# Parameters loaded as rows and turned by VectorE, and phases of three loads and three stores, in a batch normalisation that streams 1 GB

## The chip, the cores and the metric

The kernel runs on one core of one Trainium2 chip. SyncE, ScalarE, VectorE and GpSimd are engines of the core that run its program; the profile calls them SP, ACT, DVE and POOL. The data are moved by sixteen DMA engines, which work off what SyncE, ScalarE and GpSimd put on their queues. The metric is the device time of an execution in microseconds (us), lower is better. The span that the profile gives is about 2 us shorter than the measured time of the same execution.

## The reference

```python
# x: 32 x 256 x 128 x 128 float32; gamma, beta, running_mean, running_var: 256 float32
return gamma * (x - mean) / np.sqrt(var + eps) + beta      # parameters broadcast over the channel axis
```

With scale = gamma / sqrt(var + eps) and shift = beta - mean * scale it is one multiply and one add for each element. 537 MB are read and 537 MB written.

## The kernel before

A tile is 128 channels by 16384 elements, 8.39 MB, 64 KB in each partition. There are 64 tiles and three buffers. All big loads and stores are issued from SyncE's queue in the order of the program. A load waits until the store out of its buffer has landed, and a store waits for VectorE.

```python
for i in range(NBUF):            # NBUF = 3
    issue_load(i)                # nc.sync.dma_start(out=t, in_=xr[i])

def load_param(ap_1d):           # four of these, on GpSimd's queue
    t = params.tile([P, NCB], mybir.dt.float32, tag=ap_1d.tensor.name)
    nc.gpsimd.dma_start(out=t, in_=ap_1d.rearrange("(j p) -> p j", p=P))
    return t
# ... sqrt on ScalarE, reciprocal, two multiplies and a subtract on VectorE: scale_t, shift_t ...

# compute(i): nc.vector.tensor_scalar in place, t = t * scale_t + shift_t
K = NBUF - 1                     # two
for b in range((NT + K - 1) // K):
    idxs = [i for i in range(K * b, K * b + K) if i < NT]
    for i in idxs:
        compute(i)
    for i in idxs:
        store(i)
    for i in idxs:
        issue_load(i + NBUF)
```

So the queue carries three loads and then, again and again, two stores and two loads.

Of the kernel before, what the change touches and what calls it, by code (L numbers as in the profile page):

```python
# [1 line left out]

# [4 lines left out]


SINGLE_QUEUE = True  # L10
NBUF = 3


@with_exitstack
def kernel(
    ctx: ExitStack,
    tc: tile.TileContext,
    x: bass.AP,
    gamma: bass.AP,
    beta: bass.AP,  # L20
    running_mean: bass.AP,
    running_var: bass.AP,
    out: bass.AP,
):
    nc = tc.nc
    eps = 1e-5

    N, C, H, W = x.shape
    P = nc.NUM_PARTITIONS
    assert C % P == 0  # L30
    NCB = C // P
    HW = H * W
    NT = N * NCB

    params = ctx.enter_context(tc.tile_pool(name="params", bufs=1))
    data = ctx.enter_context(tc.tile_pool(name="data", bufs=NBUF))

    xr = x.rearrange("n (cb p) h w -> (n cb) p (h w)", p=P)
    outr = out.rearrange("n (cb p) h w -> (n cb) p (h w)", p=P)

    tiles = {}
    loads = {}

    def issue_load(i):
        if i >= NT:
            return
        t = data.tile([P, HW], mybir.dt.float32, tag="t")
        loads[i] = nc.sync.dma_start(out=t[:], in_=xr[i])  # L48
        tiles[i] = t

    for i in range(NBUF):
        issue_load(i)

    def load_param(ap_1d):
        t = params.tile([P, NCB], mybir.dt.float32, tag=ap_1d.tensor.name)
        nc.gpsimd.dma_start(out=t, in_=ap_1d.rearrange("(j p) -> p j", p=P))  # L56
        return t

    var_t = load_param(running_var)
    gamma_t = load_param(gamma)  # L60
    beta_t = load_param(beta)
    mean_t = load_param(running_mean)

    eps_t = params.tile([P, 1], mybir.dt.float32, tag="eps")
    nc.vector.memset(eps_t, eps)  # L65

    scale_t = params.tile([P, NCB], mybir.dt.float32, tag="scale")
    shift_t = params.tile([P, NCB], mybir.dt.float32, tag="shift")
    tmp_t = params.tile([P, NCB], mybir.dt.float32, tag="tmp")

    nc.scalar.activation(  # L71
        out=tmp_t[:],
        in_=var_t[:],
        func=mybir.ActivationFunctionType.Sqrt,
        bias=eps_t[:],
        scale=1.0,
    )
    nc.vector.reciprocal(out=tmp_t[:], in_=tmp_t[:])  # L78
    nc.vector.tensor_mul(out=scale_t[:], in0=gamma_t[:], in1=tmp_t[:])  # L79
    nc.vector.tensor_mul(out=tmp_t[:], in0=mean_t[:], in1=scale_t[:])  # L80
    nc.vector.tensor_sub(out=shift_t[:], in0=beta_t[:], in1=tmp_t[:])  # L81

    def compute(i):
        t = tiles[i]
        cb = i % NCB
        nc.vector.tensor_scalar(  # L86
            out=t[:],
            in0=t[:],
            scalar1=scale_t[:, cb : cb + 1],
            scalar2=shift_t[:, cb : cb + 1],  # L90
            op0=mybir.AluOpType.mult,
            op1=mybir.AluOpType.add,
        )

    def store(i):
        t = tiles.pop(i)
        (nc.sync if SINGLE_QUEUE else nc.scalar).dma_start(out=outr[i], in_=t[:])  # L97

    K = NBUF - 1
    for b in range((NT + K - 1) // K):  # L100
        idxs = [i for i in range(K * b, K * b + K) if i < NT]
        for i in idxs:
            compute(i)
        for i in idxs:
            store(i)
        for i in idxs:
            issue_load(i + NBUF)


# [1 line left out]
_INS = ['x', 'gamma', 'beta', 'running_mean', 'running_var']  # L111
_OUTS = [((32, 256, 128, 128), 'float32')]


# [23 lines left out]
```

## Time and profile before

| what | value | where it is read |
|---|---|---|
| time, median of 3 runs | 2491.8 us | timed runs, 2489.71 to 2493.32 |
| span of the profiled execution | 2488.1 us | head of the page |
| data queue's share of 16 DMA engines | 99.8% | queue table |
| VectorE busy | 564.7 us, 23% | busy table |
| VectorE waiting for loads | 1867.9 us | groups by line |

The following lines are from the page of the kernel before. The first two give a DMA queue's packets, MB and share of 16 engines. The last is the group of the big VectorE operation: line, engine, operation, tiles, shapes and count; then busy us and mean ns; then idle us before it and what ended it.

```profile
q1 hardware_dynamic: 18432, 1073.75, 99.8%
q0 software_dynamic: 128, 0.00, 0.0%
...
L86 DVE TENSOR_SCALAR t<-t,scale_t,shift_t 128x16384 f32<-128x16384 f32 x64 | 564.0, 8812 | 1868.0 <-DMA t<-in_x_dram 1867.9
```

The reader should see that VectorE needs 8.8 us for each tile and waits more than three times as long as it works, while the data queue (q1) keeps all sixteen engines at work. Queue q0 carries the GpSimd parameter loads.

The start of the timeline of the kernel before; columns are start, length (us), engine, line, operation, and in brackets the idle time before it.

```profile
17.42 0.16 DVE L79 TENSOR_TENSOR scale_t<-t,tmp_t 128x2 f32<-128x2 f32 x1 [3.20 <-DMA t<-in_gamma_dram]
25.17 0.16 DVE L80 TENSOR_TENSOR tmp_t<-t,scale_t 128x2 f32<-128x2 f32 x1 [7.58 <-DMA t<-in_running_mean_dram]
...
25.56 8.81 DVE L86 TENSOR_SCALAR t<-t,scale_t,shift_t 128x16384 f32<-128x16384 f32 x1
34.40 19.06 SPq L97 DMA_DIRECT2D out_dram<-t  x2
44.28 8.81 DVE L86 TENSOR_SCALAR t<-t,scale_t,shift_t 128x16384 f32<-128x16384 f32 x1 [9.91 <-DMA t<-in_x_dram]
63.64 8.81 DVE L86 TENSOR_SCALAR t<-t,scale_t,shift_t 128x16384 f32<-128x16384 f32 x1 [10.55 <-DMA t<-in_x_dram]
```

The first big operation waits for the parameters until 25.56 us. But the store that it releases at 34.40 us stands in the queue behind loads 1 and 2, and load 2 ends at about 63.6 us. An earlier start would gain nothing. Loads 1 and 2 land 19.36 us apart.

The chain of waits of the kernel before, two pieces of it far apart (start, length, what):

```profile
82.93 38.59 DMA t<-in_x_dram
...
2409.84 38.69 DMA t<-in_x_dram
```

Between these are 30 cycles of two loads and two stores, (2409.84 - 82.93) / 30 = 77.56 us each.

### The profile page before, as it was taken

The page shows a single profiled execution, that of the slowest core. Times are in us where ns is not written, and L with a number is a line of the kernel's source. Part 1 is how long each engine was busy: PE and PEld are TensorE (multiplying, and loading weights), DVE is VectorE, ACT ScalarE, POOL GpSimd, SP SyncE. Part 2 cuts the span into 40 slices and gives each one's busy share as a digit, 9 for nine tenths or more (in the row PEclk, how much of TensorE's full clock was granted, in tenths as well). Part 3 has the DMA queues.
Part 4 walks back from the last instruction along what each step waited for, and adds up shares of the span by engine and source line. Part 5 has one row for each costly group of instructions (what it writes and reads, how often), then busy time and mean ns, then how long its engine had stood idle before and what let it go on. Part 6 is the DMA issues. An engine that isn't in the chain of part 4 may idle for free.

```text
span 2488.1 us, 378 instructions
## 1 busy us (share of the span) xinstructions
DVE 564.7 (23%) x69; ACT 1.6 (0%) x2; POOL 3.2 (0%) x8
## 2 busy tenths in 40 slices
DVE  2122211222112221122212222121221212212121
ACT  0000000000000000000000000000000000000000
POOL 0000000000000000000000000000000000000000
DMA  9999999999999999999999999999999999999998
GB/s 414 429 438 433 433 429 437 436 430 431 435 436 433 428 437 436 434 428 436 433 437 428 435 435 435 426 437 436 435 427 435 436 438 426 434 437 436 432 431 378
DMA packets 18562, 1073.77 MB, mean 432 GB/s; under 512 B 2176, under 2 KB 2176, under 8 KB 2176
## 3 DMA queue, kind: packets, MB, share of 16 engines
q1 hardware_dynamic: 18432, 1073.75, 99.8%
q0 software_dynamic: 128, 0.00, 0.0%
q14 instruction: 2, 0.02, 0.0%
HBM read 536.88 MB, written 536.87 MB: 432 GB/s over the span
## 4 chain that ended last, share of the span: by engine, by line
DMA 51%; another core or an unknown queue 36%; DVE 11%; SPq 0%; issue 0%; POOL 0%; DVEq 0%; POOLq 0%; PEldq 0%
DMA t<-in_x_dram 48%; DVE t L86 11%; DMA out_dram<-t 2%; DMA t<-in_running_mean_dram 1%; SPq L97 0%; POOL t L56 0%; DVEq L86 0%; POOLq L133 0%; SPq L48 0%; DVE shift_t L81 0%; DVE tmp_t L80 0%; DVEq L80 0%; PEldq L133 0%
## 5 line engine op out<-in xcount | busy, mean ns | idle before, releaser
L86 DVE TENSOR_SCALAR t<-t,scale_t,shift_t 128x16384 f32<-128x16384 f32 x64 | 564.0, 8812 | 1868.0 <-DMA t<-in_x_dram 1867.9
L78 DVE RECIPROCAL tmp_t<-tmp_t 128x2 f32<-128x2 f32 x1 | 0.2, 166 | 13.2 <-ACT tmp_t L71 13.2
L80 DVE TENSOR_TENSOR tmp_t<-t,scale_t 128x2 f32<-128x2 f32 x1 | 0.2, 160 | 7.6 <-DMA t<-in_running_mean_dram 7.6
L71 ACT ACT_TABLE_LOAD x1 | 1.3, 1283 | 12.4 <-DMA t<-in_running_var_dram 12.4
L79 DVE TENSOR_TENSOR scale_t<-t,tmp_t 128x2 f32<-128x2 f32 x1 | 0.2, 160 | 3.2 <-DMA t<-in_gamma_dram 3.2
L56 POOL DMA_DIRECT2D t<-in_running_var_dram x1 | 0.8, 839 | 0.8 <-PEq L133 0.8
L56 POOL DMA_DIRECT2D t<-in_gamma_dram x1 | 0.7, 722 | 0.0
L56 POOL DMA_DIRECT2D t<-in_beta_dram x1 | 0.7, 722 | 0.0
L56 POOL DMA_DIRECT2D t<-in_running_mean_dram x1 | 0.7, 722 | 0.0
L71 ACT ACTIVATE tmp_t<-t,eps_t 128x2 f32<-128x2 f32 x1 | 0.3, 295 | 0.0
L65 DVE MEMSET eps_t<- 128x1 f32 x1 | 0.1, 59 | 0.8 <-PEq L122 0.8
L81 DVE TENSOR_TENSOR shift_t<-t,tmp_t 128x2 f32<-128x2 f32 x1 | 0.2, 160 | 0.0
L122 POOL MEMSET const-bfloat16-1.0<- 128x1 bf16 x1 | 0.1, 96 | 0.0
L122 POOL MEMSET const-uint8-127<- 128x1 uint8 x1 | 0.1, 94 | 0.0
L122 POOL MEMSET const-float32-0.0<- 128x1 f32 x1 | 0.1, 93 | 0.2 <-issue 0.2
L122 POOL MEMSET const-float32-1.0<- 128x1 f32 x1 | 0.1, 93 | 0.0
## 6 DMA issues: line engine op xcount, KB each, us to landing
t<-in_x_dram SPq DMA_DIRECT2D x64, 38.6
out_dram<-t SPq DMA_DIRECT2D x64, 49.9
t<-in_running_var_dram POOLq DMA_DIRECT2D x1, 1.0 KB, 11.1
t<-in_gamma_dram POOLq DMA_DIRECT2D x1, 1.0 KB, 15.2
t<-in_beta_dram POOLq DMA_DIRECT2D x1, 1.0 KB, 19.5
t<-in_running_mean_dram POOLq DMA_DIRECT2D x1, 1.0 KB, 21.6
```

The source lines that it names most:

```text
L56: nc.gpsimd.dma_start(out=t, in_=ap_1d.rearrange("(j p) -> p j", p=P))
L65: nc.vector.memset(eps_t, eps)
L71: nc.scalar.activation(out=tmp_t[:], in_=var_t[:], func=mybir.ActivationFunctionType.Sqrt, bias=eps_t[:], scale=1.0,)
L78: nc.vector.reciprocal(out=tmp_t[:], in_=tmp_t[:])
L79: nc.vector.tensor_mul(out=scale_t[:], in0=gamma_t[:], in1=tmp_t[:])
L80: nc.vector.tensor_mul(out=tmp_t[:], in0=mean_t[:], in1=scale_t[:])
L81: nc.vector.tensor_sub(out=shift_t[:], in0=beta_t[:], in1=tmp_t[:])
L86: nc.vector.tensor_scalar(out=t[:], in0=t[:], scalar1=scale_t[:, cb : cb + 1], scalar2=shift_t[:, cb : cb + 1], op0=mybir.AluOpType.mult, ...
L122: nc = _bacc.Bacc("TRN2", target_bir_lowering=False, num_devices=1)
```

## The change

It has two intents. The parameters shall no longer come as scattered 4-byte elements through GpSimd's queue, but as four rows of 1 KB on ScalarE's queue, which VectorE then turns into columns. And the queue shall change between reading and writing less often: three loads, three stores. A manual schedule keeps the program's order on each engine. The diff, cut to its core:

```diff
-SINGLE_QUEUE = True
 NBUF = 3
+GROUPS = [3] * 20 + [2, 2]
+AHEAD = 0
...
+    ctx.enter_context(tc.manual_schedule())
...
-    for i in range(NBUF):
-        issue_load(i)
-    def load_param(ap_1d):
-        t = params.tile([P, NCB], mybir.dt.float32, tag=ap_1d.tensor.name)
-        nc.gpsimd.dma_start(out=t, in_=ap_1d.rearrange("(j p) -> p j", p=P))
-        return t
+    rows = params.tile([B, C], f32, tag="rows")          # B = 32, C = 256
+    nc.vector.memset(rows, 0.0)
+    for r, ap in enumerate((running_var, gamma, beta, running_mean)):
+        nc.scalar.dma_start(out=rows[r : r + 1, :], in_=ap.rearrange("(o c) -> o c", o=1))
+    for i in range(AHEAD + GROUPS[0]):
+        load(i)
...
+    turned = params.tile([B, C], f32, tag="turned")
+    nc.vector.transpose(out=turned[:], in_=rows[:])
+    par = params.tile([P, NCB, 4], f32, tag="par")
+    blocks = turned.rearrange("p (cb q r) -> p cb q r", cb=NCB, q=NQ)
+    for q in range(NQ):
+        nc.vector.tensor_copy(out=par[q * B : (q + 1) * B], in_=blocks[:, :, q, 0:4])
...
-    K = NBUF - 1
-    for b in range((NT + K - 1) // K):
-        idxs = [i for i in range(K * b, K * b + K) if i < NT]
+    first = 0
+    for g, size in enumerate(GROUPS):
+        idxs = range(first, first + size)
         for i in idxs:
             compute(i)
         for i in idxs:
             store(i)
-        for i in idxs:
-            issue_load(i + NBUF)
+        first += size
+        more = GROUPS[g + 1] if g + 1 < len(GROUPS) else 0
+        for i in range(first + AHEAD, min(first + AHEAD + more, NT)):
+            load(i)
```

More of the change, by code (lines that the diff above doesn't have):

```diff
@@ L26 @@
     eps = 1e-5
+    f32 = mybir.dt.float32
     N, C, H, W = x.shape
@@ L33 @@
     NT = N * NCB
+    B = 32
+    NQ = P // B
+    assert sum(GROUPS) == NT and max(GROUPS) <= NBUF
     params = ctx.enter_context(tc.tile_pool(name="params", bufs=1))
@@ L39, with load @@
     outr = out.rearrange("n (cb p) h w -> (n cb) p (h w)", p=P)
+    ctx.enter_context(tc.manual_schedule())
     tiles = {}
-    loads = {}
-    def issue_load(i):
-        if i >= NT:
-            return
-        t = data.tile([P, HW], mybir.dt.float32, tag="t")
-        loads[i] = nc.sync.dma_start(out=t[:], in_=xr[i])
-        tiles[i] = t
-    for i in range(NBUF):
-        issue_load(i)
-    def load_param(ap_1d):
-        t = params.tile([P, NCB], mybir.dt.float32, tag=ap_1d.tensor.name)
-        nc.gpsimd.dma_start(out=t, in_=ap_1d.rearrange("(j p) -> p j", p=P))
-        return t
-    var_t = load_param(running_var)
-    gamma_t = load_param(gamma)
-    beta_t = load_param(beta)
-    mean_t = load_param(running_mean)
-    eps_t = params.tile([P, 1], mybir.dt.float32, tag="eps")
-    nc.vector.memset(eps_t, eps)
-    scale_t = params.tile([P, NCB], mybir.dt.float32, tag="scale")
-    shift_t = params.tile([P, NCB], mybir.dt.float32, tag="shift")
-    tmp_t = params.tile([P, NCB], mybir.dt.float32, tag="tmp")
+    def load(i):
+        t = data.tile([P, HW], f32, tag="t")
+        nc.sync.dma_start(out=t[:], in_=xr[i])
+        tiles[i] = t
+    rows = params.tile([B, C], f32, tag="rows")
[4 more added lines that the diff above has]
+        load(i)
+    eps_t = params.tile([P, 1], f32, tag="eps")
+    nc.vector.memset(eps_t, eps)
+    turned = params.tile([B, C], f32, tag="turned")
[4 more added lines that the diff above has]
+        nc.vector.tensor_copy(out=par[q * B : (q + 1) * B], in_=blocks[:, :, q, 0:4])
+    var_t, gamma_t, beta_t, mean_t = (par[:, :, r] for r in range(4))
+    scale_t = params.tile([P, NCB], f32, tag="scale")
+    shift_t = params.tile([P, NCB], f32, tag="shift")
+    tmp_t = params.tile([P, NCB], f32, tag="tmp")
     nc.scalar.activation(
         out=tmp_t[:],
-        in_=var_t[:],
+        in_=var_t,
         func=mybir.ActivationFunctionType.Sqrt,
@@ L78 @@
     nc.vector.reciprocal(out=tmp_t[:], in_=tmp_t[:])
-    nc.vector.tensor_mul(out=scale_t[:], in0=gamma_t[:], in1=tmp_t[:])
-    nc.vector.tensor_mul(out=tmp_t[:], in0=mean_t[:], in1=scale_t[:])
-    nc.vector.tensor_sub(out=shift_t[:], in0=beta_t[:], in1=tmp_t[:])
+    nc.vector.tensor_mul(out=scale_t[:], in0=gamma_t, in1=tmp_t[:])
+    nc.vector.tensor_mul(out=tmp_t[:], in0=mean_t, in1=scale_t[:])
+    nc.vector.tensor_sub(out=shift_t[:], in0=beta_t, in1=tmp_t[:])
     def compute(i):
@@ L96, in store @@
         t = tiles.pop(i)
-        (nc.sync if SINGLE_QUEUE else nc.scalar).dma_start(out=outr[i], in_=t[:])
-    K = NBUF - 1
-    for b in range((NT + K - 1) // K):
-        idxs = [i for i in range(K * b, K * b + K) if i < NT]
+        nc.sync.dma_start(out=outr[i], in_=t[:])
+    first = 0
+    for g, size in enumerate(GROUPS):
+        idxs = range(first, first + size)
         for i in idxs:
```

## The prediction

> **What bounds the kernel now.** The sixteen DMA engines, all the time. The queue table gives the data queue 99.8% of 16 engines' span, at a mean of 432 GB/s; VectorE is 23% busy and its 1868 us of idle time wait for loads (groups by line). In the timeline loads 1 and 2 release VectorE 19.36 us apart (44.28, 63.64), and an undisturbed 64 KB packet takes 2.418 us in the DMA records, so one 8.39 MB transfer is 8 x 2.418 = 19.34 us, 434 GB/s. The Trainium skill, "DMA: Bandwidth & Descriptors", section "Where 436 GB/s comes from", puts the fabric's ceiling at 435.2 GB/s; the trace agrees. 128 transfers are at least 2476 us of the 2488.1 us span. Only 12 us are anything else.
>
> **Where those 12 us are** (packet records, followed engine by engine): 3 us before the first packet; then the slowest engine falls 9.1 us behind 1024 undisturbed packets. Of this 3.2 us come during load 0, where 64-byte parameter packets, some taking 0.5 to 1.0 us, mix with the load; the other 6 us come slowly, nearly all in the last packet of a load before a store or the first packet of that store: 32 changes, 0.19 us each on the slowest engine. In the chain of waits the cycle of two loads and two stores lasts 77.56 us on average (82.93 to 2409.84 in 30 cycles) against 77.38 us for 32 packets.
>
> **What the change does.**
> - Parameters: four GpSimd loads, the last landing 21.6 us after issue, become four 1 KB rows on ScalarE's queue. VectorE gains a memset, a transpose and four copies: estimated 2 us in all, from 0.16 us for its small operations, done before load 0 lands. The first big operation, held until 25.56 us by the parameters, may start 2 us earlier, but its store queues behind loads 1 and 2 (until about 63 us): worth nothing. Only fewer small packets beside load 0 are worth something: estimated 1.2 of the 3.2 us.
> - Phases of three: no hole if the queue never runs dry. Store 2 of a group is issued 9 us after its load lands (8.81 us of VectorE), with stores 0 and 1, 38 us of work, ahead of it; each next load is issued when its buffer's store lands, mostly with 19 us or more ahead. In the groups of two at the end one transfer is still ahead. So nothing is lost, and load-to-store changes fall from 32 to 22: 10 x 0.19 = 1.9 us saved. The tail (load, two stores) is the same.
> - The manual schedule keeps the order of emission, which the old trace has already.
>
> All saving is on the critical path, but small: 3.1 us. Span 2488.1 to 2485; time 2491.8 to 2488.7. A gain over 2% (below 2442 us) would need more than 434 GB/s; a loss over 2% would need holes of 2.3 us per group.
>
> **What would show it.** DMA queue share above 99%; six transfers in about 116.3 us (floor 116.06); the 64 KB packet still 2.418 us; VectorE idle 1868 us, waiting for loads; first big operation at about 23 us; lateness in load 0 near 2 us.
>
> **What would make it wrong.** A hole where loads follow stores, if a store's completion comes over 19 us after its data; row loads disturbing load 0 as much as before; a change's cost growing with the length of a phase; run-to-run spread (3.6 us among three runs), as large as the effect.
>
> Predicted 2488.7 us, 2484.5 to 2492 (8 in 10); faster by over 2%: 0.01, within 2%: 0.98, slower: 0.01.

## The result, and the profile after

| set | before, median (runs) | changed, median (runs) | ratio, 95% interval |
|---|---|---|---|
| first result | 2490.76 us (6) | 2486.14 us (6) | 0.9988, 0.9977 to 0.9999 |
| second | 2487.48 us (9) | 2487.54 us (5) | 0.9997, 0.9984 to 1.0009 |
| third | 2487.42 us (9) | 2486.85 us (5) | 0.9996, 0.9983 to 1.0008 |

A ratio is from the runs of the same rounds, so it is not quite the ratio of the medians in the table (the plain means of the runs in a set give 0.9985, 0.9997 and 0.9996). By ratio the gain is 3.0 us in the first set (0.0012 x 2490) and 0.7 to 1.0 us in the two others, whose intervals include no gain at all. All together, 24 runs of the kernel before have a mean of 2488.4 us and a standard deviation of 2.2 us; 16 runs of the changed kernel 2486.7 us and 0.9 us. The predicted 2488.7 us is 2.6 us above the first measured median, and the range of 2484.5 to 2492 holds it.

The lines of the changed kernel that answer to those shown above, first from its page:

```profile
q1 hardware_dynamic: 18432, 1073.75, 99.9%
...
q10 hardware_dynamic: 8, 0.00, 0.0%
...
L93 DVE TENSOR_SCALAR t<-t,scale_t,shift_t 128x16384 f32<-128x16384 f32 x64 | 564.0, 8812 | 1863.9 <-DMA t<-in_x_dram 1863.8
```

Nothing of the balance has moved: the same VectorE work, the same waiting for loads, the data queue at 99.9%. Queue q10 is ScalarE's; its 8 packets are four rows and four completions.

The start of its timeline (SPq and ACTq are the queues that issue DMAs):

```profile
0.73 1.33 SPq L51 DMA_DIRECT2D t<-in_x_dram  x3
...
2.20 0.35 ACTq L58 DMA_DIRECT2D rows<-in_running_mean_dram  x1
...
22.65 0.43 DVE L66 STREAM_TRANSPOSE turned<-rows 32x256 f32<-32x256 f32 x1 [21.53 <-DMA rows<-in_running_mean_dram]
23.12 0.69 DVE L71 COPY par<-turned 32x8 f32<-32x8 f32 x4
...
24.95 8.81 DVE L93 TENSOR_SCALAR t<-t,scale_t,shift_t 128x16384 f32<-128x16384 f32 x1
33.80 37.81 SPq L104 DMA_DIRECT2D out_dram<-t  x3
41.92 8.81 DVE L93 TENSOR_SCALAR t<-t,scale_t,shift_t 128x16384 f32<-128x16384 f32 x1 [8.16 <-DMA t<-in_x_dram]
62.43 8.81 DVE L93 TENSOR_SCALAR t<-t,scale_t,shift_t 128x16384 f32<-128x16384 f32 x1 [11.70 <-DMA t<-in_x_dram]
```

The row loads are issued by 2.5 us, but the last row lands only at about 22.6 us, so the first big operation starts at 24.95 us, hardly earlier than the 25.56 us of before. And loads 1 and 2 release VectorE 20.51 us apart (41.92 to 62.43), where before it was 19.36 us. That is 1.2 us lost in one place, which the experiments below look into.

The chain of waits of the changed kernel, the same piece of two cycles far apart (its "unknown queue" piece spans a whole phase of stores and the load after it):

```profile
71.24 68.50 another core or an unknown queue
...
2278.84 68.35 another core or an unknown queue
```

19 cycles of three loads and three stores lie between, (2278.84 - 71.24) / 19 = 116.19 us each. I had predicted 116.3.

### How far each DMA engine falls behind

The views above can't show a loss of a fraction of a microsecond on single engines. For that I used the trace's own record of every packet. A 64 KB packet is followed on its engine by another that starts when it ends, so the 16384 big packets can be joined into sixteen chains of 1024. The undisturbed step is 2.414 us from start to start. "Lateness" is how far a packet starts after (its number) x 2.418 us from the first packet of the kernel, the scale I had used before I predicted. (2.418 us is the length of a packet's record, a little more than the step. With the mean undisturbed step of 2.4153 us, completions between transfers included, 1024 packets are 2473.3 us, so that about 15 us of the first span lay above them and not the 12 us of the prediction; a comparison of kernels is the same on either scale.) The joining is mine and not the profiler's; packets that cross at nearly the same time can be exchanged between chains, so sums over all engines are firmer than one engine's.

Worked out so, in us, with the span from each page:

```
run                 changes  slowest engine at the last packet   span     span minus lateness
before                  32       9.1                            2488.1      2479.0
after                   22       4.4                            2483.6      2479.2
after, second run       22       5.2                            2484.5      2479.3
after, third run        22       4.7                            2483.9      2479.2
e1_rows_only            32       6.0                            2485.3      2479.3
e2_phases_only          22       5.7                            2484.7      2479.0
e3_phases_of_one        63       6.3                            2485.6      2479.3
```

A "change" is a point where the stream goes from loads to stores. The last column is the same within 0.3 us in all seven: it is 1024 x 2.418 = 2476.0 us and 3 us more, which in the kernel before are 1.8 us before the first packet and 1.2 us after the last (the prediction put all 3 us before the first packet). What differs between these kernels is therefore just how late their slowest engine is, and one can ask where that lateness comes from. Note also that the only profile of the kernel before comes from one of its slower executions: the median of all 24 of its runs is 2487.6 us.

### The profile page after: what moved, and what is told of

Its sections match the earlier page's. It is cut to its first block, busy times and chain, and to the rows that moved or that the text cites. A ratio compares the mean times of both kernels' runs of the same rounds, so it can differ in the third digit from the quotient of the medians.

```text
span 2483.6 us, 383 instructions
## 1 busy us (share of the span) xinstructions
DVE 566.0 (23%) x75; ACT 1.6 (0%) x2; POOL 0.2 (0%) x4
## 3 DMA queue, kind: packets, MB, share of 16 engines
q1 hardware_dynamic: 18432, 1073.75, 99.9%
## 4 chain that ended last, share of the span: by engine, by line
another core or an unknown queue 72%; DVE 22%; DMA 4%; issue 0%; DVEq 0%; SPq 0%
DVE t L93 22%; DMA t<-in_x_dram 4%; DVEq L93 0%; SPq L51 0%; SPq L104 0%
```

## The experiments

The theory that I went in with (A): the row parameters save about 1.2 us in load 0, and each change from loads to stores costs about 0.19 us on the slowest engine, so that fewer changes save 1.9 us. Rivals: the gain is all of one half; and (D) the loss is no price per change at all but a drift of the sixteen engines against each other, which stops once they are far enough apart.

The table is worked out from the packet records. It sums, for each stretch of the run, what packets lost beyond the undisturbed step (only losses above 60 ns), as a mean over the sixteen engines, in us:

```
run                     changes  load 0  first   82 to   650 to   1250 to  1850 to   sum after
                                         change  650 us  1250 us  1850 us  2480 us  first change
before                     32     2.09    0.00    1.02    1.33     0.77     0.94       4.06
e1_rows_only               32     0.67    1.11    2.58    0.80     0.02     0.04       3.44
e2_phases_only             22     2.27    0.00    0.79    0.97     0.50     0.51       2.77
after                      22     0.59    1.22    0.27    0.90     0.61     0.39       2.17
after, second run          22     0.73    1.07    0.90    1.55     0.26     0.51       3.22
after, third run           22     0.71    1.05    0.75    1.04     0.75     0.60       3.14
e3_phases_of_one           63     0.66    1.11    2.67    0.47     0.08     0.05       3.27
e5_half_tiles_of_one      125     0.59     *      3.38    0.00     0.11     0.05       3.54
e6_first_sbuf_read         22     0.69    1.04    1.85    1.83     0.66     0.71       5.05
e7_first_dram_write        22     0.66    1.09    0.66    1.21     0.32     0.39       2.58
e8_rows_before_loads       22     0.75    1.33    1.21    0.88     0.27     0.39       2.75
e9_small_load              22     0.53    0.91    1.30    1.17     0.65     0.14       3.26
e10_eight_engines_late     22     1.86    0.00    1.08    1.71     0.64     0.56       3.99
```

The stretches are us of the trace's record, which starts some 9 us before the span. In e5 the star stands for changes that lie before 82 us and that I didn't separate. The kernels e6 to e10 are explained below; each of them was run once. That kernels with the same 22 changes lose between 2.2 and 5.1 us after the first one is the scatter against which differences in this table have to be seen.

### The changed kernel again, and its two halves

after_again is the changed kernel as it is.

> The changed kernel once more, beside its two halves. Expected as in the first result: about 3 to 4.5 us faster than before (ratio 0.9982 to 0.9990), span near 2484 us, first big operation at about 25 us, last parameter row landing about 21 us after its issue.

Measured: 2487.54 us, ratio 0.9997 (0.9984 to 1.0009). The gain was smaller than expected and not clear of zero; the parameter row and the first big operation were where I expected them.

e1_rows_only keeps the old loop with its phases of two and takes the rows (told in short, not the literal diff):

```diff
-    var_t = load_param(running_var)        # and three more, on GpSimd's queue
+    rows = params.tile([B, C], f32, tag="rows")   # four rows on ScalarE's queue, transpose, four copies
     K = NBUF - 1                                  # loop of the kernel before
```

> The parameters as rows, with the old phases of two. My prediction (parameters worth 1.2 us, phases 1.9 us): 1 to 2 us faster than before, and 2 us slower than the changed kernel; the slowest engine's lateness after load 0 about 1 us instead of 3.2. Rival 'it is all the parameters': as fast as the changed kernel. Rival 'it is all the phases': as slow as before.

Measured: 2487.15 us, ratio 0.9996 (0.9982 to 1.0010). Lateness after load 0 on the slowest engine was 1.2 us, as expected (before: 3.2).

e2_phases_only keeps the changed kernel's loop and takes back the GpSimd loads (again in short):

```diff
-    rows = params.tile([B, C], f32, tag="rows")   # and what follows from it
+    var_t = load_param(running_var)               # and three more, as before
     GROUPS = [3] * 20 + [2, 2]                    # loop of the changed kernel
```

> Phases of three with the four GpSimd parameter loads of the kernel before. My prediction: about 2 us faster than before, 1 to 2 us slower than the changed kernel; lateness after load 0 about 3 us as before; loss at load-to-store changes 3 us or less on the slowest engine instead of 6. Rival 'all parameters': as before. Rival 'all phases': as the changed kernel.

Measured: 2486.75 us, ratio 0.9996 (0.9983 to 1.0008). Lateness after load 0 was 5.0 us on the slowest engine, later than expected.

What follows: the two halves and the whole can't be told apart by time; all three are within 0.05% of the kernel before in these rounds. The packet records can tell. The losses before and in the first change are the interesting ones. With GpSimd's parameter loads (before, e2) load 0 costs the engines 2.1 to 2.3 us and the first change nothing. With rows (e1, the changed kernel) load 0 costs about 0.65 us and the first change 1.1 us, on all sixteen engines. So most of what the rows save in load 0, about 1.5 us, is given back 40 us later. That is where the expected gain of the parameters went.

### Many more changes

e3_phases_of_one, phases of one load and one store, with one load issued further ahead so that the queue always has work:

```diff
-GROUPS = [3] * 20 + [2, 2]
-AHEAD = 0
+GROUPS = [1] * 64
+AHEAD = 1
```

> The changed kernel with phases of one load and one store: 64 load-to-store changes instead of 22, one load more issued ahead so that the queue doesn't run dry. If every change costs 0.1 to 0.19 us on the slowest engine (my prediction), 4 to 8 us slower than the changed kernel (about 2490 to 2494 us). Rival: the loss is a drift of the engines against each other that comes to rest at some 6 to 9 us whatever the number of changes: at most 3 us slower than the changed kernel.

(There are 63 such changes, for the first two loads stand together.) Measured: 2487.53 us, ratio 1.0000 (0.9988 to 1.0013), beside 2487.54 us of the changed kernel in the same rounds (the means are 2488.04 and 2487.24 us). Theory A asked for 4 to 8 us more. Nearly three times as many changes cost nothing that can be measured, so a price per change falls. In the table the losses of e3 come early: 2.67 us until 650 us, then 0.47, 0.08 and 0.05 us. By then the engines have moved apart and hardly lose anything more. e1, with 32 changes, shows the same end: 0.02 and 0.04 us in the last two stretches. The changed kernel, with only 22, is still losing 0.4 to 0.6 us in the last stretch.

That the losses end is measured in these kernels; that it is the distance between the engines which ends them (theory D) is not shown. The distance can be read without my chains, from the sixteen completion packets of one transfer. In e1 they lie 4.9 us apart from 1250 us on, in e3 6.4 us from 650 us on, and there the losses have ended. But in the kernel before, which has as many changes as e1, they lie 6.9 us apart at 1250 us and 9.1 us at 1850 us, and its engines still lose 0.77 and 0.94 us in the last two stretches.

e5_half_tiles_of_one goes further, with half tiles (32 KB per partition), six buffers and phases of one:

```diff
-NBUF = 3
-GROUPS = [3] * 20 + [2, 2]
-AHEAD = 0
+NBUF = 6
+GROUPS = [1] * 128
+AHEAD = 3
...
-    HW = H * W
-    NT = N * NCB
+    HW = H * W // 2
+    NT = N * NCB * 2
```

> Changed kernel with tiles of half the size, six buffers and phases of one half tile: 128 load-to-store changes and 256 transfers instead of 22 and 128. The prediction's 0.19 us per change: about 20 us slower than the changed kernel. Drift that comes to rest: within 3 us of the changed kernel, the spread of the engines at most 10 us at the end, and no losses at the changes in the second half of the run.

Measured: 2492.85 us, ratio 1.0023 (1.0009 to 1.0036); the changed kernel in the same rounds had 2486.85 us. So it is 6.0 us slower: far from the 20 us that a price per change asks for, and outside the 3 us that I gave the drift. The missing part is in the packets. Its page says how many there are:

```profile
DMA packets 36877, 1073.80 MB, mean 431 GB/s; under 512 B 4100, under 2 KB 4104, under 8 KB 4104
...
q1 hardware_dynamic: 36864, 1073.76, 100.1%
```

An undisturbed 32 KB packet takes 1210.8 ns from start to start in its records, and a 64 KB packet 2415.3 ns in the changed kernel's. 2 x 1210.8 - 2415.3 = 6.3 ns are lost by cutting one packet in two, and with 1024 such packets on an engine that is 6.4 us. (Both means include the completions between transfers, of which e5 has twice as many.) I hadn't reckoned with it; it accounts for the 6.0 us. The Trainium skill, "DMA: Bandwidth & Descriptors", section "Why small descriptors are slow (HBM only)", states a fixed overhead of some 3 cycles for each packet in the DMA engine; that there is a fixed part agrees with this run, and its size here is 6.3 ns for each further packet. The losses at changes end early here too: 3.38 us before 650 us, then 0.00, 0.11 and 0.05 us.

The last column of the table is the plainest argument: after the first change, 22, 32, 63 and 125 changes lose 2.2 to 5.1 (nine kernels and runs), 3.4 to 4.1, 3.3 and 3.5 us in all.

### What the first change's 1.1 us is

Three theories: (P) each engine's first read out of SBUF costs 1.1 us once; (Q) its first write to DRAM does; (R) it is the sixteen engines doing the change at the same moment. With rows the engines are within 0.4 to 0.9 us of each other at the first change; with GpSimd loads they are 1.4 us (before) and 2.9 us (e2) apart. Each of the next three kernels puts one small DMA of 8 KB on all sixteen engines during load 0, and each was run once.

e6_first_sbuf_read:

```diff
+    seed = params.tile([P, 16], f32, tag="seed")
+    nc.vector.memset(seed, 0.0)
+    copy = params.tile([P, 16], f32, tag="copy")
+    nc.scalar.dma_start(out=copy[:], in_=seed[:])
     rows = params.tile([B, C], f32, tag="rows")
```

> Changed kernel plus one 8 KB copy from SBUF to SBUF on ScalarE's queue, on all 16 engines, during load 0. In the runs with row parameters all engines lose about 1.1 us at the first load-to-store change and at no later one; with GpSimd parameters they lose it in load 0 instead. Theory P (each engine's first read out of SBUF costs 1.1 us, once): the loss moves into load 0, lateness at packet 8 median about 2.0 us, and the first change costs less than 0.3 us. Rival Q (first write to DRAM): first change still 1.1 us. Rival R (engines in lockstep at the first change): still about 1.1 us unless this copy spreads them by over 1.4 us.

Measured: the first change still cost 1.04 us, lateness at packet 8 had a median of 0.95 us. P falls.

e7_first_dram_write:

```diff
+    scratch = nc.dram_tensor("scratch", (P, 16), f32, kind="Internal").ap()
+    nc.scalar.dma_start(out=scratch, in_=xr[0][:, 0:16])
     rows = params.tile([B, C], f32, tag="rows")
```

> Changed kernel plus one 8 KB copy from DRAM to a DRAM scratch tensor on all 16 engines during load 0. Theory P (first SBUF read): first change still costs about 1.1 us on all engines. Rival Q (first DRAM write): the loss moves into load 0 and the first change costs less than 0.3 us. Rival R (lockstep): first change about 1.1 us.

Measured: first change 1.09 us. Q falls.

e9_small_load, the control:

```diff
+    copy = params.tile([P, 16], f32, tag="copy")
+    nc.scalar.dma_start(out=copy[:], in_=xr[0][:, 0:16])
     rows = params.tile([B, C], f32, tag="rows")
```

> Control: changed kernel plus one 8 KB load from DRAM into SBUF on all 16 engines during load 0, so the small packets are there but neither an SBUF read nor a DRAM write. Theories P, Q and R: first change still about 1.1 us on all engines, load 0 nearly undisturbed. If the loss moves into load 0 here too, P and Q both fall and it is any small packet on every engine.

Measured: first change 0.91 us, load 0 0.53 us. Small packets on every engine are not it either. (In all three, the engines stayed within 0.5 to 0.9 us of each other at the first change.)

e10_eight_engines_late makes eight of the engines late by a load that they alone carry (cut: `load` uses the tiles taken here):

```diff
+    for i in range(3):                       # all three tiles taken first
+        t = data.tile([P, HW], f32, tag="t")
+        tiles[i] = t
+    nc.sync.dma_start(out=tiles[2][0:8, 0:8192], in_=xr[2][0:8, 0:8192])
     for i in range(AHEAD + GROUPS[0]):
         load(i)
```

> Changed kernel plus one extra load of 8 partitions x 32 KB ahead of load 0, which makes the lowest 8 of the 16 engines about 1.2 us late and nothing else. Only what is left of the first change's 1.1 us is asked. If it comes from the engines running in lockstep (spread 0.4 to 0.9 us in the runs that had it, 1.4 and 3.0 us in those that had not): spread at the first change about 1.6 us, and its mean loss below 0.4 us. If it belongs to the row parameters or to the missing GpSimd loads in some other way: still about 1.1 us on all engines.

Measured, in one run: the engines went through load 0 in two groups of eight, with a spread of about 1.2 us, somewhat less than I had intended. The first change cost nothing that reaches 60 ns, on any engine, also not on the eight that carried no extra packet. This is what R expected, but it doesn't show R, for the extra load did more than make eight engines late. The first packet of load 0 took 4.7 to 5.3 us on the eight engines without an extra packet and 3.2 to 4.0 us on the others, so that load 0 cost 1.86 us in the mean and not 0.5 to 0.75 us as in the other runs with rows. So a fourth theory (S) stands beside R: every engine loses this time once, in load 0 where that is disturbed enough, otherwise at the first change. In the table load 0 and the first change together make 1.4 to 2.3 us in every row that has both, with or without a loss at the change. No run has its engines apart without about 2 us lost before. Being in step isn't enough either: at the second change the changed kernel's engines were still within 0.7 us of each other and lost only 0.1 us. Which part of the chip the engines wait for the runs don't show. Nor is anything won: e10 lost 3.99 us after the first change, more than any other kernel but e6 and the one before.

e11_graded_spread was to start the engines up to 9.7 us apart:

```diff
+    nc.sync.dma_start(out=tiles[2][0:8, 0:16384], in_=xr[2][0:8, 0:16384])
+    nc.sync.dma_start(out=tiles[2][8:12, 0:16384], in_=xr[2][8:12, 0:16384])
+    nc.sync.dma_start(out=tiles[2][12:14, 0:16384], in_=xr[2][12:14, 0:16384])
+    nc.sync.dma_start(out=tiles[2][14:15, 0:16384], in_=xr[2][14:15, 0:16384])
     for i in range(AHEAD + GROUPS[0]):
         load(i)
```

> Changed kernel plus four extra loads of 64 KB rows on 8, 4, 2 and 1 engines ahead of load 0, so that the engines start up to 9.7 us apart. If the losses at the changes are a drift that ends once the engines are far enough apart: they are small from the beginning, the mean loss per engine at all changes together below 1.7 us (3.4 to 4.4 us in the row-parameter runs so far), and the spread stays near 10 us. If every change has its price whatever the spread: mean loss about 3 us or more again.

It worked in part only. The loads were held until 11.99 us, and the extra packets took up to 9.0 us each instead of 2.4, so that this kernel needed 2510.88 us. (The first packets of load 0, on twelve engines, took 7.2 to 7.9 us as well; why is not shown.) The completions of its first big load show twelve engines still together and four later by 2.0 to 12.8 us. With that spread the first change cost nothing, also on the twelve engines that were within 0.25 us of each other there. So R doesn't hold for twelve engines in step, and S, for which load 0 was disturbed enough, is not contradicted.

The stretches to 1850 us lost 0.07, 0.30 and 0.24 us: 0.6 us in sum, where the changed kernel's three runs lost 1.8 to 2.7 us. In the last stretch my chains of engines cross; the lengths of the packets alone, which need no chains, show 1.0 us lost there, 0.8 of it between 2380 and 2480 us. Small losses from the beginning are what theory D expected. But eleven engines stayed within 0.4 us of each other until near the end and hardly lost anything, so this run doesn't show that distance is what spares an engine. It is one run of a kernel disturbed at its start, and it is weaker evidence than e3 and e5.

### Why the rows land so late

e8_rows_before_loads puts the rows on the loads' own queue, ahead of them:

```diff
     for r, ap in enumerate((running_var, gamma, beta, running_mean)):
-        nc.scalar.dma_start(out=rows[r : r + 1, :], in_=ap.rearrange("(o c) -> o c", o=1))
+        nc.sync.dma_start(out=rows[r : r + 1, :], in_=ap.rearrange("(o c) -> o c", o=1))
```

> Changed kernel with the four rows issued on the loads' own queue, ahead of load 0. If the late landing (21 us) of the rows comes only from taking turns with 64 KB packets on one engine (8 turns of 2.43 us), the rows now land before 6 us after the start, and the first big operation waits for load 0 alone and starts at about 24 us (load 0 starts 1 to 2 us later, for the row issues stand before it). Time: 1 to 2 us more than the changed kernel, since only the start of the loads counts. Rival (a row load with a slow path of its own): rows still land after 10 us.

Measured, in one run: 2489.24 us, beside one run of the kernel before of 2486.45 us. Its timeline:

```profile
2.09 0.24 SPq L58 DMA_DIRECT2D rows<-in_running_mean_dram  x1
2.38 1.30 SPq L51 DMA_DIRECT2D t<-in_x_dram  x3
3.46 0.43 DVE L66 STREAM_TRANSPOSE turned<-rows 32x256 f32<-32x256 f32 x1 [2.34 <-DMA rows<-in_running_mean_dram]
...
5.57 0.16 DVE L88 TENSOR_TENSOR shift_t<-par,tmp_t 128x2 f32<-128x2 f32 x1
24.29 8.81 DVE L93 TENSOR_SCALAR t<-t,scale_t,shift_t 128x16384 f32<-128x16384 f32 x1 [18.55 <-DMA t<-in_x_dram]
```

The rows are there at 3.46 us and the parameters ready at 5.7 us, so the row loads have no slow path of their own. In the changed kernel they are slow since they take turns. The packet records of its queue q10 show a row, its completion, the next row and so on at 16.10, 18.56, 20.98, 23.43, 25.85, 28.31, 30.73 and 33.19 us of the trace's record: eight turns, one every 2.4 us, each after one 64 KB packet of load 0 on the same engine. The Trainium skill, "DMA: Bandwidth & Descriptors", section "Queues, rings and completion order", says that an engine goes round its queues and changes only at packet boundaries; the trace agrees. It also shows what this means for a small transfer beside 64 KB packets: 1 KB takes two turns, almost 5 us. Each row is one packet on one engine.

The early parameters gain nothing. The first big operation then waits for load 0, and load 0 is issued at 2.38 instead of 0.73 us. That delay is on the critical path: the span of 2487.5 us less the slowest engine's 6.6 us is 2480.9 us, 1.6 to 1.9 us more than in the seven runs above.

## Why the prediction was right or wrong

**Right: what bounds the kernel, and that little could change.** The sixteen engines are busy 99.8% and 99.9% of the span. The Trainium skill, "DMA: Bandwidth & Descriptors", section "Where 436 GB/s comes from", states 435.2 GB/s as the fabric's ceiling; the undisturbed packet here, 16 x 65536 bytes in 2.4153 us, is 434.1 GB/s. With the 12 us that I had counted beyond the packets (about 15 on the measured step), neither a gain nor a loss of 2% was in reach.

**Right: no holes, and the tail is the same.** 116.19 us for six transfers against a predicted 116.3 us; VectorE's waiting fell by 4 us.

**Right in the sum, by luck.** "3.1 us" of saving was predicted and 3.0 us by ratio measured in the first set, but 0.7 and 1.0 us in the two later ones. I had costed the loss from one profiled execution whose slowest engine was 9.1 us late; the span minus the lateness is the same in seven runs, and typical runs of the kernel before are faster than that one. The two later sets can't tell the gain from nothing. That the first set shows the predicted 3 us is luck: the sum was made of a saving that was mostly given back and of a price that doesn't exist.

**Wrong: the parameter work "done before load 0 lands" and "first big operation at about 23 us".** The last row landed at 22.6 us, and the operation started at 24.95 us. I had overlooked the turns that a row takes with 64 KB packets. It cost no time, as the prediction said that this start is worth nothing.

**Wrong in its account: "estimated 1.2 of the 3.2 us".** The slowest engine's lateness in load 0 fell from 3.2 to 1.1 us, more than the "near 2 us" predicted. But at the first change the changed kernel then lost 1.2 us in the mean, which none of its engines escaped and which the kernel before doesn't lose there. At packet 24, after it, the slowest engine is 2.4 us late against 3.3 before: 0.9 us is left. Why it is given back stays open between R and S.

**Wrong: "32 changes, 0.19 us each on the slowest engine" and "10 x 0.19 = 1.9 us saved".** This is the step that failed in its mechanism. I had divided 6 us by 32 and taken the quotient for a price. e3 has 63 changes and the time of the changed kernel; e5 has 125, and its 6.0 us are those of its smaller packets. What the runs showed instead is a sum of 2 to 5 us for each engine after the first change, which doesn't grow with the number of changes; in the kernels with the most changes (e3, e5) and in e1 it is spent by 1250 us. The place of the losses was seen rightly (the last packet of a load before a store), the law was not. What ends the losses, where they end, is not shown. A part of the scatter of the kernel before (standard deviation 2.2 against 0.9 us) may lie in how late one engine happens to drift; that is argued and not shown, for there is only one profile of it. If its span less its lateness were 2479.2 us in its other executions too, the 18 further spans (2483.7 to 2489.3 us) would mean 4.5 to 10.1 us for the slowest engine, and the changed kernel's 16 spans (2483.3 to 2486.1 us) 4.1 to 6.9 us; this is an estimate.

What stays open: which shared part makes a load's last packet wait near a change to stores, why the first change costs 1.1 us in some kernels and nothing in others and so much more than the second, what ends the losses in e1, e3 and e5 but not in the kernel before, and whether the changed kernel gains 0.7 or 3 us. No kernel that was run is clearly better than the changed one: its span is 2479.2 us plus the slowest engine's 4 to 5 us.

## What to carry to other kernels

When the DMA engines are busy for 99.8% of the span at the ceiling of their rate, compute the floor first (here 128 transfers of 19.3 us) and accept that reordering can only win what lies above it. A loss that is found at certain events isn't yet a price per event: double or triple the number of events, as e3 and e5 do, before you multiply. And small loads that must come early belong ahead of the big ones, at the price of a later start of these (1.65 us in e8), or on a path where waiting is harmless; beside 64 KB packets each row and each completion waited a turn of 2.4 us. When a disturbance is used to test a theory, look at all that it disturbed: e10's extra load was to make eight engines late and cost all sixteen time in load 0.

## What the Trainium skill lacked or had wrong

- "DMA: Bandwidth & Descriptors" describes turns at packet boundaries but not the resulting delay: here a 1 KB row and its completion each waited for one 64 KB packet, 2.4 us a turn, and four rows took about 20 us.
- The same page illustrates its fixed cost per packet with a small descriptor and has no figure for packets of tens of KB. Going from 64 KB to 32 KB packets cost 6.3 ns for each further packet, 6 us in 2487.
- No page has the losses of the sixteen engines near changes from loads to stores: about 1.1 us on all of them at the first change in the nine profiles whose load 0 had cost 0.5 to 0.75 us, nothing there in before, e2 and e10, whose load 0 had cost 1.9 to 2.3 us; then 2.2 to 5.1 us in the mean, whether 22 or 125 changes follow.
- "HBM Reference", section "Specifications (TRN2)", gives about 425 GB/s for a core that streams alone; this kernel has 432 GB/s over the span and 434 GB/s in undisturbed packets, with loads and stores mixed.
